# Layer 1's output projection as plain fp32 products, with stationary widths of 128, 64 and 32 columns

## The chip, the cores and the metric

The kernel runs on one core of one Trainium2 chip. The metric is the device time of one execution in microseconds (us); the time before is the median of two runs, 1154.54 us. The core's engines are named PE (TensorE, with its weight loads as a row of their own, PEld), DVE (VectorE), ACT (ScalarE), POOL (GpSimd) and SP (SyncE, whose queue issues the DMA transfers here).

## The reference, cut to what matters

Two layers of a diffusion backbone work on 512 latent and 256 context tokens of width 1024. Each layer runs two attention branches (a neighbourhood attention and a grouped-query attention) on one modulated input, gates their outputs, merges them and projects the result back:

```python
def _merge(a_att, b_att, a_z, b_z, g_a, g_b, w_o_a, w_o_b, w_out):
    o_a = (a_att * jax.nn.silu(a_z)) @ w_o_a
    o_b = (b_att * jax.nn.silu(b_z)) @ w_o_b
    merged = jax.nn.sigmoid(g_a) * o_a + jax.nn.sigmoid(g_b) * o_b
    return merged @ w_out
...
    x_new = x + gate_x * out_x
```

The change touches `merged @ w_out` of layer 1, the last layer. There only the 512 latent tokens are left: a product of 512 x 1024 by 1024 x 1024, and after it the gate and the residual sum, which is the kernel's output. All inputs are fp32.

## The kernel before, in words

Nearly all large products are done in three passes on split operands. A tile is split into `hi`, the tile rounded to the fp32r type, and `lo`, the rest; `mm3` (lines 339 to 343) then adds hi x hi, hi x lo and lo x hi in PSUM, each as a matmul of fp32r operands. The first operand of `T.matmul` after the output is the stationary one (128 rows by up to 128 columns), the second is the moving one (128 by 512 here). The sum over the 1024 inputs is made of KT = 8 steps of 128, the k tiles.

Weights come through `load_w` (lines 303 to 316): for every k tile a DMA on SP's queue (line 309) into one of three staging buffers `raw`, a cast on ACT into `whi` (line 311), and a subtraction into `wlo` (line 314), alternately on POOL and DVE for this projection (`mix_lo`). `whi` and `wlo` have 8 buffers each.

A token projection, `tok_proj` (called for each tile of 128 tokens), takes a PSUM tile of 128 x 512, runs `tok_mm` (lines 345 to 349) over the 8 k tiles with the token tile of the activations as the stationary operand and a weight tile as the moving one, and hands the result to an evacuation function.

The end of a layer stands from line 981 on:

- The projection of branch b (`o_chunks("b", ...)`), in four chunks of 256 output channels. Its weights are split tiles too and use the same `whi` and `wlo` buffers. Its evacuation `evac_b` gates the product (line 993), adds branch a (line 994), and splits the sum into the tiles `mh` (a cast on ACT, line 996) and `ml` (a subtraction on DVE, line 997). These are the merged activations, with the channels on the partitions; `mg` holds them, four channel tiles in each pair of large buffers (`big`, 9 buffers of 128 x 3072).
- The residual tiles `xt` are loaded (line 1013; four in layer 1).
- The output projection: for each half `n` of the 1024 output columns, the weights `w_out` are loaded, and for each token tile `t` (6 in layer 0, 4 in layer 1) `tok_proj` runs. The evacuation `evac_o` multiplies by the gate (line 1025) and adds the residual (line 1027) on DVE; in layer 1 the result goes to the output by a DMA (line 1029).

The order of instructions on each engine is set by a scheduler that simulates a timeline when the kernel is built: instructions that are ready in its timeline may be moved ahead of others that still wait, so products of neighbouring token tiles can be interleaved. PSUM tiles of 512 columns come from two pools, `psf` (one buffer) and `psx` (five buffers at this stage).

One place of the kernel already uses plain fp32 matmuls: `ada_part` (from line 185) computes layer 0's modulation. Its products, line 190, have a stationary tile `scol` of 32 columns and a moving weight tile of 512; four of them, each with its own k tile, go to four quarters of the partitions of one PSUM tile:

```python
        for h, w in enumerate(ws):
            for j in range(4):
                T.matmul(pt[32 * j:32 * j + 32], scol[:, 4 * h + j, :], w[:, j, :], start=h == 0, stop=h == 1)
```

`ada_part` is called four times, with 8 matmuls each. Line 655 and its neighbours transpose fp32 tiles of 128 x 128 on PE, by a product with an identity.

Of the kernel before, what the change touches and what calls it, by code (L numbers as in the profile page):

```python
# [7 lines left out]
F32 = mybir.dt.float32  # L8
# [3 lines left out]
ALU = mybir.AluOpType  # L12
# [9 lines left out]
KT = DM // 128  # L22
# [17 lines left out]
def R(ap):  # L40
    return ap.bitcast(F32R)


def F(ap):
    return ap.bitcast(F32)
# [3 lines left out]
def hybrid_kernel(es: ExitStack, tc, x, ctx, cvec, w_ada, w_ada0, small, gvec, w_in, w_o_a, w_o_b, w_out,  # L49
                  bias_int, bias_edge, rope, ident_d, out):  # L50
    nc = tc.nc
    V, S, G, T = nc.vector, nc.scalar, nc.gpsimd, nc.tensor
# [3 lines left out]
    wp = es.enter_context(tc.tile_pool(name="wp", bufs=8))  # L56
# [6 lines left out]
    def nm(s):  # L63
        uid[0] += 1
        return f"{s}_{uid[0]}"

    def big(name):
        return bigp.tile([128, 3072], F32, tag="big", name=nm(name))
# [12 lines left out]
    def open_ps(x=0, **kinds):  # L81

        if "es" in pm:
            pm["es"].close()
        pm["es"] = ExitStack()
        pm["n"], pm["i"] = x + 1, 0
        if x:
            kinds["x"] = (x, 512)
        for kind, (bufs, cols) in kinds.items():
            ps_pool(pm["es"], kind, bufs, cols)  # L90

    def psw(n=512, kind="w"):
        if kind == "w":
            kind = "f" if pm["i"] % pm["n"] == 0 else "x"
            pm["i"] += 1
        pool, cols = pm[kind]
        return pool.tile([128, cols], F32, tag=kind, name=nm("ps" + kind))[:, :n]
# [9 lines left out]
    def x_src(t):  # L107
        if t < 4:
            return x0[128 * t:128 * t + 128, :]
        return ctx0[(t - 4) * 128:(t - 3) * 128, :]  # L110
# [52 lines left out]
    def raw_tile():  # L163
        return wp.tile([128, 512], F32, tag="raw", name=nm("raw"), bufs=3)
# [67 lines left out]
    def ada_mod(l):  # L232
        mod_finish(l, ada_sum(0, 16, 2).rearrange("p (a k) v -> p a k v", a=2), 0, 8)
# [69 lines left out]
    def load_w(src, col0, n, nk, lo_eng, k0=0, own=None, bufs=8):  # L303

        pool, x = (wp, "") if own is None else (own, "x")
        res = []
        for k in range(k0, k0 + nk):
            raw = raw_tile()
            nc.sync.dma_start(raw[:, :n], src[128 * k:128 * k + 128, col0:col0 + n])
            hi = pool.tile([128, 512], F32R, tag="whi" + x, name=nm("whi"), bufs=bufs)  # L310
            S.copy(hi[:, :n], raw[:, :n])  # L311
            lo = pool.tile([128, 512], F32R, tag="wlo" + x, name=nm("wlo"), bufs=bufs)
            e = lo_eng(k)
            e.tensor_tensor(lo[:, :n], raw[:, :n], F(hi[:, :n]), ALU.subtract)  # L314
            res.append((hi, lo))
        return res

    def load_w2(src, col0, nk, lo_eng):

        res = []  # L320
        for i in range(nk // 2):
            raw = raw_tile()
            nc.sync.dma_start(raw.rearrange("p (k n) -> p k n", k=2),
                              src[256 * i:256 * i + 256, col0:col0 + 256].rearrange("(k p) n -> p k n", k=2))
            hi = wp.tile([128, 512], F32R, tag="whi", name=nm("whi"), bufs=8)
            S.copy(hi, raw)  # L326
            lo = wp.tile([128, 512], F32R, tag="wlo", name=nm("wlo"), bufs=8)
            lo_eng(i).tensor_tensor(lo, raw, F(hi), ALU.subtract)  # L328
            res += [(hi[:, c:c + 256], lo[:, c:c + 256]) for c in (0, 256)]
        return res  # L330

    pool_lo = lambda k: G
    bq_lo = lambda k: G if k % 4 == 0 else V
    mix_lo = lambda k: V if k % 2 == 1 else G
# [10 lines left out]
    def tok_mm(ps, w, n, a, t, k0, k1):  # L345
        for k in range(k0, k1):
            hi, lo = a(0, k), a(1, k)
            mm3(ps, (R(hi[:, 128 * t:128 * t + 128]), R(lo[:, 128 * t:128 * t + 128])),
                (w[k][0][:, :n], w[k][1][:, :n]), k == 0, k == KT - 1)

    def tok_proj(w, n, a, t, evac):

        ps = psw(n)
        tok_mm(ps, w, n, a, t, 0, KT)
        evac(t, ps)
        turn_late(hp["lag"])
# [31 lines left out]
    def turn_late(n):  # L388

        while len(hp["late"]) > n:  # L390
            behind(ON_PE, hp["late"].pop(0))

    def run(fill, n):
        for _ in range(min(n, len(fill))):
            fill.pop(0)()
# [80 lines left out]
    def layer(l, hx, nxt, mid):  # L476
        first = l == 0
# [59 lines left out]
        def hilo_tiles(name):  # L537
            return [big(name + part).rearrange("p (f n) -> p f n", f=4) for part in "hl"]

        def hilo(src, dst, fs):  # L540
            sv = src.rearrange("p (f n) -> p f n", f=4)
            for f in fs:
                S.copy(R(dst[0][:, f, :ntok]), sv[:, f, :ntok])
                G.tensor_tensor(R(dst[1][:, f, :ntok]), sv[:, f, :ntok], dst[0][:, f, :ntok], ALU.subtract)
# [28 lines left out]
        def tg_part(c, f, n0, n1):  # L573
            return tg[2 * (f // 4) + c].rearrange("p (f n) -> p f n", f=4)[:, f % 4, n0:n1]
# [7 lines left out]
        if first:  # L582
            w, pss = [], [psw() for t in range(6)]
# [19 lines left out]
        else:  # L603
            hp["p"] = bgp_es.enter_context(tc.tile_pool(name=f"cp{l}", bufs=1, reuse_waits="tile"))
            w = load_w(W, C_AK, 512, KT, mix_lo)
# [6 lines left out]
        w = load_w(W, C_AV, 512, KT, mix_lo)  # L612
# [5 lines left out]
        w = load_w(W, C_AQ, 512, KT, mix_lo, own=hp["p"])  # L618
# [17 lines left out]
        if True:  # L636
# [262 lines left out]
            w = load_w2(W, C_BKV, KT, mix_lo)  # L899
# [81 lines left out]
        with tc.tile_pool(name=f"mrg{l}", bufs=1, reuse_waits="tile") as mp:  # L981
            open_ps(x=5)
            extra = lambda name: mp.tile([128, 3072], F32, tag="extra", name=nm(name))
            gv = mp.tile([128, nv, DM], F32, tag="gate", name=nm("gate"), bufs=1)
            for v in range(nv):
                src = gd[l][8 * v:8 * v + 8].rearrange("k p -> (k p)").unsqueeze(0)
                nc.sync.dma_start(gv[:, v, :], src.to_broadcast([128, DM]))
            hilo(zb, gated["b"], [3])
            mg = []

            def evac_b(f, n0, n1, ps):
                a, b = tg_part(0, f, n0, n1), tg_part(1, f, n0, n1)
                V.scalar_tensor_tensor(b, b, 1.0, ps, ALU.add, ALU.mult)
                V.tensor_tensor(a, a, b, ALU.add)
                hi, lo = [m[:, f % 4, n0:n1] for m in mg[f // 4]]
                S.copy(R(hi), a)
                V.tensor_tensor(R(lo), a, hi, ALU.subtract)
            chunks = o_chunks("b", None, evac_b)
            chunks[0][0]()
            for i in range(4):  # L1000
                if i < 3:
                    chunks[i + 1][0]()
                if i % 2 == 0:
                    mg.append(hilo_tiles("m"))
                for piece in chunks[i][1]:
                    piece()

            nt = 6 if first else 4
            xv = [a.rearrange("p (t n) -> p t n", t=3) for a in (big("xt0"), extra("xt1"))]
            xts = []  # L1010
            for t in range(nt):
                xt = xv[t // 3][:, t % 3, :]
                nc.sync.dma_start(xt, x_src(t) if first else xs1[128 * t:128 * t + 128, :])
                xts.append(xt)
            a_m = lambda part, k: mg[k // 4][part][:, k % 4, :]
            bg = ada_steps(1, range(16), (1,), 2, mp) + [lambda: ada_mod(1)] if first else []
            run(bg, 1)
            per_bg = -(-len(bg) // nt)
            for n in range(2):
                w = load_w(w_out[l], 512 * n, 512, KT, mix_lo)  # L1020

                def evac_o(t, ps, n=n):
                    cs = slice(512 * n, 512 * n + 512)
                    t1 = mp.tile([128, 512], F32, tag="t1", name=nm("t1"), bufs=2)
                    V.tensor_tensor(t1, ps, gv[:, 0 if t < 4 else 1, cs], ALU.mult)
                    xt = xts[t]
                    V.tensor_tensor(xt[:, cs], xt[:, cs], t1, ALU.add)
                    if not first:
                        nc.sync.dma_start(o_lat[16 * t:16 * t + 16][:, :, cs], xt[:, cs])
                    elif n == 1:  # L1030
                        if t < 4:
                            nc.sync.dma_start(xs1[128 * t:128 * t + 128, :], xt)
                        late.append(lambda: make_hx(1, t, xt, nxt(), mp))
                late = []
                for t in range(nt):
                    tok_proj(w, 512, a_m, t, evac_o)
                    run(bg, per_bg)
                    run(late, len(late) - 1)
                run(late, len(late))
# [102 lines left out]
```

## Time and profile before

| | |
|---|---|
| runs | 1154.26 and 1154.82 us, median 1154.54 |
| profiled execution: span from the first to the last instruction | 1153.4 us (the page gives no other time of this execution) |
| span against the median of the runs | 1.1 us less |
| PE busy | 1123.0 us, 97% of the span |
| DVE, ACT, POOL busy | 809.8, 573.9, 495.0 us |
| mean granted TensorE clock | 0.998 |
| changed stage, from its first product to the end of its last | 1104.34 to 1147.86 us of the span, 43.52 us |
| tail after it | 5.54 us |

How to read it: a row of the profile names line, engine, operation and tiles (`psx<-wlo,mh` is a write to a PSUM tile that reads `wlo` and `mh`, which of them is stationary isn't said), then the stationary shape (128*128) and the moving one (128x512). Matmuls are pipelined: one starts before the one ahead of it has ended, and their ends are modelled. So a matmul's duration is not what it adds to the time; the distance from one start to the next is. A stretch is written from:to in microseconds from the span's start. All types are shown as f32 where a matmul's operand is fp32 or fp32r; the line tells which it is.

### The profile page before, as it was taken

The numbers are of one execution on the slowest core, as the hardware profiler recorded it, in microseconds if no ns is written. First come the engines' busy times: TensorE is split into PE (matmuls) and PEld (weight loads), VectorE is DVE, ScalarE is ACT, GpSimd is POOL, SyncE is SP. The second block draws the span as 40 slices with busy tenths as digits, with TensorE's granted clock in tenths as the row PEclk, the third lists the DMA queues.
The fourth block names the chain that finished last, engine by engine and source line by source line (L and its number), as shares of the span: only waits on it lengthen the run. The fifth ranks groups of instructions, "written<-read, shape, count | busy, mean of one in ns | idle before, by whom it ended". The sixth has DMA issues, their size and how long they took to land.

```text
span 1153.4 us, 17280 instructions
## 1 busy us (share of the span) xinstructions
PE 1123.0 (97%) x6078; PEld 949.0 (82%) x6078; DVE 809.8 (70%) x1508; ACT 573.9 (50%) x1167; POOL 495.0 (43%) x459
## 2 busy tenths in 40 slices
PE   5999999999999999999999999999999999999998
PEld 4688888889988888878788787888888988887786
DVE  4566688897464687688587755469787665898563
ACT  5453266666433465566330265346666445766521
POOL 3362354454375243354411126245553664465311
PEclk9999999999999999999999999999999999999999
DMA  9644222233342332470353523543332333142143
GB/s 368 195 126 137 69 85 65 72 115 97 115 130 63 107 102 73 67 276 19 121 172 101 174 74 110 176 106 113 108 105 84 110 101 101 65 173 92 63 129 92
DMA packets 88000, 134.04 MB, mean 116 GB/s; under 512 B 10629, under 2 KB 52585, under 8 KB 86249
## 3 DMA queue, kind: packets, MB, share of 16 engines
q1 hardware_dynamic: 87912, 132.94, 36.8%
q8 instruction: 48, 0.79, 0.3%
q14 instruction: 40, 0.32, 0.1%
HBM read 115.58 MB, written 17.32 MB: 115 GB/s over the span
## 4 chain that ended last, share of the span: by engine, by line
PE 83%; DVE 7%; issue 3%; POOL 2%; ACT 2%; DMA 2%; ACTq 0%; POOLq 0%; DVEq 0%
PE psx L341 12%; PE psx L343 12%; PE psx L342 12%; PE psf L341 9%; PE psf L342 9%; PE psf L343 9%; PE pst L655 5%; PE pss L704 2%; PE pss L705 2%; PE psv L959 2%; PE psv L958 1%; PE pss L781 1%; PE pst L417 1%; DVE wlo L328 1%; DVE ptl L659 1%
## 5 line engine op out<-in xcount | busy, mean ns | idle before, releaser
L659 DVE TENSOR_TENSOR ptl<-pst,pth 128x512 fp32r<-128x512 f32 (+1 forms) x176 | 116.0, 672 | 46.4 <-ACT pth L658 45.4
L658 ACT CAST pth<-pst 128x512 fp32r<-128x512 f32 (+1 forms) x176 | 99.2, 576 | 87.5 <-PE pst L655 56.3
L328 POOL TENSOR_TENSOR wlo<-raw,whi 128x512 fp32r<-128x512 f32 x68 | 95.0, 1402 | 108.9 <-ACT whi L326 87.8
L341 PE MATMUL psf<-hx,whi 128*128 128x512 f32 (+1 forms) x368 | 139.2, 378 | 0.0
L342 PE MATMUL psf<-hx,whi 128*128 128x512 f32 (+1 forms) x368 | 138.1, 375 | 0.0
L343 PE MATMUL psf<-hx,wlo 128*128 128x512 f32 (+1 forms) x368 | 137.8, 374 | 0.0
L341 PE MATMUL psx<-whi,hx 128*128 128x512 f32 (+1 forms) x368 | 137.2, 374 | 0.0
L342 PE MATMUL psx<-wlo,hx 128*128 128x512 f32 (+1 forms) x368 | 135.8, 369 | 0.0
L343 PE MATMUL psx<-whi,hx 128*128 128x512 f32 (+1 forms) x368 | 133.6, 369 | 0.0
L314 POOL TENSOR_TENSOR wlo<-raw,whi 128x512 fp32r<-128x512 f32 x44 | 60.4, 1373 | 140.4 <-ACT whi L311 123.8
L311 ACT CAST whi<-raw 128x512 fp32r<-128x512 f32 x96 | 58.7, 623 | 103.5 <-PE psx L343 38.6
L326 ACT CAST whi<-raw 128x512 fp32r<-128x512 f32 x136 | 82.5, 622 | 50.3 <-DMA raw<-in_w_in_dram 34.1
L655 PE MATMUL pst<-ident,p 128*128 128x128 f32 x640 | 99.9, 272 | 1.4 <-DVE ptl L659 0.9
L328 DVE TENSOR_TENSOR wlo<-raw,whi 128x512 fp32r<-128x512 f32 x68 | 70.2, 1033 | 28.3 <-ACT whi L326 27.8
L655 PEld LDWEIGHTS pst<-ident,p 128*128 128x128 f32 x640 | 77.7, 141 | 13.3 <-DVE ptl L659 1.6
L644 POOL TENSOR_SCALAR r<-r 128x1 f32<-128x1 f32 x64 | 23.1, 361 | 151.7 <-DVE r L639 144.1
L645 POOL TENSOR_TENSOR p<-p,r 128x512 f32<-128x512 f32 (+1 forms) x64 | 83.5, 1304 | 5.0
L341 PEld LDWEIGHTS psx<-whi,hx 128*128 128x128 f32 x368 | 69.6, 189 | 11.8 <-issue 0.8
L343 PEld LDWEIGHTS psf<-hx,wlo 128*128 128x128 f32 x368 | 69.4, 188 | 11.8
L343 PEld LDWEIGHTS psx<-whi,hx 128*128 128x128 f32 x368 | 69.4, 189 | 11.5
L342 PEld LDWEIGHTS psx<-wlo,hx 128*128 128x128 f32 x368 | 69.6, 189 | 11.0
L341 PEld LDWEIGHTS psf<-hx,whi 128*128 128x128 f32 x368 | 69.4, 189 | 10.8 <-ACT zt L502 0.2
(239 smaller groups left out, 3033.4 us busy)
## 6 DMA issues: line engine op xcount, KB each, us to landing
raw<-in_w_in_dram SPq DMA_DIRECT2D x168, 256.0 KB, 2.9
rawb<-in_w_ada_dram SPq DMA_DIRECT2D x64, 256.0 KB, 2.8
gs<-zt SPq DMA_DIRECT2D x32, 256.0 KB, 2.0
raw<-in_w_out_dram SPq DMA_DIRECT2D x32, 256.0 KB, 2.8
tg<-gs SPq DMA_DIRECT2D x4, 1536.0 KB, 7.4
rawx<-in_w_ada_dram SPq DMA_DIRECT2D x4, 1024.0 KB, 7.2
rawy<-in_w_ada_dram SPq DMA_DIRECT2D x4, 1024.0 KB, 12.2
raw<-in_w_o_a_dram SPq DMA_DIRECT2D x16, 256.0 KB, 2.7
```

Source lines behind the costliest of these rows:

```text
L311: S.copy(hi[:, :n], raw[:, :n])
L314: e.tensor_tensor(lo[:, :n], raw[:, :n], F(hi[:, :n]), ALU.subtract)
L326: S.copy(hi, raw)
L328: lo_eng(i).tensor_tensor(lo, raw, F(hi), ALU.subtract)
L341: T.matmul(ps, lhs[0], rhs[0], start=first, stop=False)
L342: T.matmul(ps, lhs[0], rhs[1], start=False, stop=False)
L343: T.matmul(ps, lhs[1], rhs[0], start=False, stop=last)
L644: G.tensor_scalar(r[:, i:i + 1], r[:, i:i + 1], 0.5, None, ALU.mult)
L645: G.tensor_tensor(p[:, c0:c1], p[:, c0:c1], r[:, i:i + 1].to_broadcast([128, c1 - c0]), ALU.mult)
L655: T.transpose(pt[:, c0:c0 + 128], src, ident)
L658: S.copy(hi[:, n0:n1], pt[:, n0:n1])
L659: V.tensor_tensor(lo[:, n0:n1], pt[:, n0:n1], F(hi[:, n0:n1]), ALU.subtract)
```

## The change

In layer 1 (`first` is false) alone:

- `evac_b` writes the merged sum as one fp32 tile `mf`, with one DVE instruction, and does not split it. `mg` holds one large buffer for four channel tiles in place of two.
- `load_full` loads the weights of the output projection as plain fp32 tiles, straight by DMA into the buffers of the tags `wlo` (even k) and `whi` (odd k). Nothing is staged, cast or subtracted.
- `full_mm` replaces `tok_proj` in the loop over the token tiles. For each k tile it runs one plain fp32 matmul for each group of `cols` stationary columns, into the partitions of PSUM that belong to these tokens. `cols` is 128 for token tile 0, 64 for tile 1 (two groups), 32 for tiles 2 and 3 (four groups each).

Layer 0 is as before. The evacuation `evac_o`, the residual loads and the output transfers are unchanged.

```diff
+    def load_full(src, col0, n, nk):
+
+        res = []
+        for k in range(nk):
+            w = wp.tile([128, 512], F32, tag="whi" if k % 2 else "wlo", name=nm("wf"), bufs=8)
+            nc.sync.dma_start(w[:, :n], src[128 * k:128 * k + 128, col0:col0 + n])
+            res.append(w)
+        return res
+
+    def full_mm(ps, w, n, a, t, cols):
+        for k in range(KT):
+            for c in range(0, 128, cols):
+                T.matmul(ps[c:c + cols], a(k)[:, 128 * t + c:128 * t + c + cols], w[k][:, :n],
+                         start=k == 0, stop=k == KT - 1)
...
             def evac_b(f, n0, n1, ps):
                 a, b = tg_part(0, f, n0, n1), tg_part(1, f, n0, n1)
                 V.scalar_tensor_tensor(b, b, 1.0, ps, ALU.add, ALU.mult)
+                if not first:
+                    V.tensor_tensor(mg[f // 4][:, f % 4, n0:n1], a, b, ALU.add)
+                    return
...
-                    mg.append(hilo_tiles("m"))
+                    mg.append(hilo_tiles("m") if first else big("mf").rearrange("p (f n) -> p f n", f=4))
...
-                w = load_w(w_out[l], 512 * n, 512, KT, mix_lo)
+                w = (load_w if first else load_full)(w_out[l], 512 * n, 512, KT, *[mix_lo][:first])
...
-                    tok_proj(w, 512, a_m, t, evac_o)
+                    if first:
+                        tok_proj(w, 512, a_m, t, evac_o)
+                    else:
+                        ps = psw(512)
+                        full_mm(ps, w, 512, lambda k: mg[k // 4][:, k % 4, :], t, (128, 64, 32, 32)[t])
+                        evac_o(t, ps)
```

## The prediction

> **What bounds the kernel now.** I read the head of the page first, then the busy time in three stretches: the end of the projection before the changed one, the changed projection itself (layer 1's output projection), and the tail.
>
> ```profile
> span 1153.4 us, 17280 instructions
> PE 1123.0 (97%) x6078; PEld 949.0 (82%) x6078; DVE 809.8 (70%) x1508; ACT 573.9 (50%) x1167; POOL 495.0 (43%) x459
> PE 83%; DVE 7%; issue 3%; POOL 2%; ACT 2%; DMA 2%; ACTq 0%; POOLq 0%; DVEq 0%
> ...
> 1084.74:1104.34 19.60, 19.60 (x89) 16.17 (x87) 14.11 (x21) 8.67 (x15) 7.17 (x6) 1.00 0.26 83
> 1104.34:1147.86 43.52, 43.52 (x193) 35.85 (x191) 18.90 (x27) 6.96 (x12) 6.47 (x5) 1.00 0.42 127
> 1147.86:1153.40 5.54, 0.16 (x1) 0.00 (x0) 1.38 (x2) 0.00 (x0) 0.00 (x0) 0.88 0.18 47
> ```
>
> The columns of the stretches are: width, then busy time with count of PE, PEld, DVE, ACT and POOL, the granted clock, the DMA share, GB/s. PE carries 83% of the chain of work that ended last, and in the changed stage PE is busy for 43.52 of 43.52 us at clock 1.00. Nothing there waits for data, DVE has 18.90 us of work and ACT 6.96. So one thing sets the time of this stage: how long TensorE needs for its products. Time that the change saves on ACT, DVE or POOL in this stage is not on the path. The products of the stage, by form:
>
> ```profile
> L342 PE MATMUL psx<-wlo,mh 128*128 128x512 f32 x56 | 21.6, 389 | 0.0
> L343 PE MATMUL psx<-whi,ml 128*128 128x512 f32 x56 | 21.6, 389 | 0.0
> L341 PE MATMUL psx<-whi,mh 128*128 128x512 f32 x56 | 21.5, 389 | 0.0
> ...
> 1145.59 0.39 PE L343 MATMUL psx<-whi,ml 128*128 128x512 f32 x1
> ...
> 1146.27 0.39 PE L343 MATMUL psx<-whi,ml 128*128 128x512 f32 x1
> ```
>
> Each line has 8 more in the other PSUM pool, which makes 3 x 64 = 192 (the stretch counts 193, one of them the tail of the stage before): 2 halves of the output columns, 4 token tiles, 8 k tiles, three passes. A matmul's 389 ns is not its price, because the next one starts before it ends; the price is the distance between starts. Three passes of one k tile take 1146.27 - 1145.59 = 0.68 us, so one takes 0.2267 us, and 192 take 43.5 us: the width of the stage.
>
> **What a plain fp32 product costs.** The kernel has such a product already. Line 190, in layer 0's modulation, multiplies two plain fp32 tiles, 32 stationary columns by 512 moving ones, four such groups side by side in one PSUM tile. That is the form of the third and fourth token tiles after the change. Its rows (four calls of the part, 8 calls of matmul in each):
>
> ```profile
> L190 PE MATMUL pst<-rawx,scol x32: 592/605/617, 12.9 to 47.6; 128*32 128x512 f32 x32
> L190 PE MATMUL pst<-rawy,scol x32: 592/592/593, 13.8 to 48.5; 128*32 128x512 f32 x32
> ...
> 30.10 0.40 PE L343 MATMUL psx<-whi,hx 128*128 128x512 f32 x1
> 30.42 0.64 PE L190 MATMUL pst<-rawx,scol 128*32 128x512 f32 x4
> ...
> 30.88 0.61 PE L190 MATMUL pst<-rawx,scol 128*32 128x512 f32 x4
> 31.31 0.61 PE L190 MATMUL pst<-rawy,scol 128*32 128x512 f32 x4
> ...
> 32.28 0.50 PE L341 MATMUL psx<-whi,hx 128*128 128x512 f32 x1
> 32.61 0.39 PE L342 MATMUL psx<-wlo,hx 128*128 128x512 f32 x1
> ```
>
> The 32 calls left 64 records, so each call is two. Four records start together at 30.42, four at 30.88, four at 31.31: the four column groups do run side by side, and a batch takes 31.31 - 30.88 = 0.43 us. That is about two passes of 0.2267, so a k tile (two batches) takes 0.86 to 0.89 us (30.42 to 31.31). I take 0.87. The record's length says the same: 592 ns against 389 for a three-pass product, 203 ns or about one pass of 512 columns more.
>
> So grouping fills the array again, and no more than that: four groups of 32 cost what one tile of 128 should cost. Against 0.68 us for three passes, the fp32 product is the dearer one: four passes in place of three.
>
> **128 and 64 stationary columns** are not in the trace as fp32 products. The nearest row for 128 is the transposition, an fp32 operand against the fp32 identity:
>
> ```profile
> 1079.90 0.60 PE L655 MATMUL pst<-ident,p 128*128 128x128 f32 x4
> ...
> L655 PE MATMUL pst<-ident,p x12: 270/272/273, 1079.9 to 1082.6; 128*128 128x128 f32 x12
> ```
>
> Four of them take 0.60 us with a last one of 0.272, so the starts are (0.60 - 0.272) / 3 = 0.109 us apart for 128 columns: 0.437 for 512, and 0.87 for the two records of a call. Lower bound: one pass for each record, 2 x 0.2267 = 0.45. Upper bound at 128: weight loads that no longer hide. The loads of the three-pass products take 35.85 / 191 = 0.188 us each and lie beside the products now; bare, they make 2 x (0.437 + 0.188) = 1.25 us of a k tile. Upper bound at 64: two groups one after the other, 1.74. I take 0.87 for both, the row nearest to them on either side of their width. For 32 columns the lower bound is the measured 0.86; the upper one is a rate at which PE gets instructions. The closest that pairs of load and product stand for long is this:
>
> ```profile
> 420.28 0.28 PE L343 MATMUL psf<-hx,wlo 128*128 128x256 f32 x1
> 420.40 0.28 PE L341 MATMUL psf<-hx,whi 128*128 128x256 f32 x1
> ```
>
> That is 0.12 us a pair. A k tile in four groups has 8 pairs, 0.96 us at this rate; line 190 ran 8 pairs in 0.89, but only in bursts of 16 that may have been queued while PE waited.
>
> **Changes of form.** Into line 190 the step is 30.42 - 30.10 = 0.32 us where 0.227 is usual; out of it, the last batch starts at about 31.74 and the next product at 32.28, 0.54 in place of 0.43, and one more step is 0.33. That is 0.1 us going in and 0.2 coming out. The stage has six changes (three passes to 128, 128 to 64, 64 to 32, back to 128, then to 64 and 32): 6 x 0.15 = 0.9 us, with 0.6 and 1.2 as ends. The Trainium skill (TensorEngine Tiling (Array Packing), section "Key Properties") speaks against the mixing of widths: changing the tiling mode drains the engine, whereas moving between tiles of a mode doesn't. It gives no price; the rows above agree with some 0.1 to 0.2 us at each change.
>
> **What else moves.** These edits I cost at nothing, and PE's full row in the stage is what hides them.
>
> ```profile
> L311 ACT CAST whi<-raw 128x512 fp32r<-128x512 f32 x16 | 9.9, 621 | 22.5 <-PE psx L343 11.5 <-DMA raw<-in_w_out_dram 8.4 <-PE psx L342 2.5
> L314 POOL TENSOR_TENSOR wlo<-raw,whi 128x512 fp32r<-128x512 f32 x8 | 11.1, 1388 | 32.9 <-ACT whi L311 32.9
> L314 DVE TENSOR_TENSOR wlo<-raw,whi 128x512 fp32r<-128x512 f32 x8 | 6.0, 749 | 11.9 <-ACT whi L311 11.9
> L997 DVE TENSOR_TENSOR ml<-tg,mh 128x512 fp32r<-128x512 f32 x8 | 6.6, 835 | 0.7 <-ACT mh L996 0.7
> L996 ACT CAST mh<-tg 128x512 fp32r<-128x512 f32 x8 | 5.0, 623 | 8.9 <-DVE tg L994 5.8 <-issue 3.0
> ```
>
> All of these go: 9.9 + 5.0 us of ACT, 11.1 of POOL, 6.0 + 6.6 of DVE. For each merged channel tile a cast and a subtraction (0.62 and 0.68 us or more) vanish ahead of its first use, so the last one is ready some 1.5 us sooner. Nothing is won by that, since PE had other products to do and did not idle. It is needed later, too: the last k tile of the first token tile comes 7 x 0.87 = 6.1 us after the stage's start. Should that cover fail, a late tile costs one or two microseconds.
>
> The 16 weight transfers of 256 KB stay. They land in the 8 + 8 buffers of the split weights and no longer in three staging buffers, so they wait for the products of the projection before, in place of a conversion:
>
> ```profile
> 1090.81 12.85 SPq L309 DMA_DIRECT2D raw<-in_w_out_dram  x6
> 1103.71 1.37 SPq L1013 DMA_DIRECT2D xt<-xs  x3
> ...
> raw<-in_w_out_dram SPq DMA_DIRECT2D x13, 256.0 KB, 3.0
> ```
>
> That projection runs 96 products, 21.8 us, until 1104.34. The buffers of the first 8 transfers come free by its middle, about 1093.4, those of the other 8 by its end. With 3.0 us to land and some queueing, the first column half has its weights by about 1098; the second has them by about 1110 and needs them 28 us after 1104.34. The four residual tiles (512 KB each) and the eight output transfers are as before, and the tail, from the last product over two DVE instructions to the output's landing, stays at 5.54 us: the last batch of four groups ends together, and its evacuation is the old one.
>
> **The sum.** Removed: 43.5 us. Added: 64 k tiles x 0.87 = 55.7, changes of form 0.9. The span goes from 1153.4 to 1153.4 - 43.5 + 55.7 + 0.9 = 1166.5 us. The page gives no time for its execution but the span; the median of the two runs, 1154.54, lies 1.1 above it, so I add 1.1: **1167.6 us**, 13.1 us or 1.1% slower.
>
> **Rivals.**
>
> *Not slower.* The 0.43 us of a batch could be the price of four streams of moving data at once, not of an fp32 record: each record one pass when it runs alone or with one neighbour. Then 128 and 64 columns cost 0.45 us a k tile and only the groups of 32 cost 0.87. One column half takes 16 x 0.45 + 16 x 0.87 = 21.1 us, both 42.2, with the changes of form 43.1 in place of 43.5: 1154.1 us. It decides at the first token tile: starts of 128 column records 0.23 us apart. For it: no such product is in the trace. Against it: a record of line 190 is itself 203 ns longer than a one-pass product, and a transposition, which has no neighbour, also takes 0.437 us for 512 columns. Chance 0.05. The Trainium skill (Perfetto Trace Analysis, section "Engine Utilization", the first note to its table) halves the array's output rate for FP32_LOW_HIGH. Read as the rate of the whole product that is 0.45 us for each k tile, an estimate that would put this rival's price on the first two token tiles; read as the rate of one of the two records it is 0.9, and line 190's 0.87 agrees with that reading only.
>
> *Two groups of 64 don't overlap.* If the 64 column form ran its groups one after the other, the second token tile would cost 16 x (1.74 - 0.87) = 13.9 us more: 1181.5. For it: no 64 column product is in the trace. Against it: four of 32 do overlap, by the same partition offsets of the output. Chance 0.09.
>
> *Late weights and mixed tiles.* If SP's queue puts the weight loads behind the three residual loads of 1103.71, the first weights land at about 1106.7 and PE waits 2.4 us; and if the order of instructions mixes token tiles of different widths, as the present one mixes tiles while merged channels are late, some 16 more changes of form cost 16 x 0.15 = 2.4: 1172.4. Chance 0.10.
>
> *Weight loads or issue bind.* Bare weight loads at 128 cost 16 x (1.25 - 0.87) = 6.1 us, and pairs at 0.12 us add 32 x (0.96 - 0.87) = 2.9 in the tiles of four groups: up to 1176.6. Chance 0.07.
>
> That the change doesn't do what it says I leave out: the diff replaces the only calls in that loop.
>
> **How the numbers follow.** The forecast has 0.69, and its own range is 1165 to 1171 (0.86 to 0.89 for each k tile, 0.6 to 1.2 for the changes of form, and a few microseconds for order). The range to hold the time is 1163 to 1178: it takes in the forecast, the mixed tiles and the weight loads (0.86 together) and leaves out the rivals at 1154.1 and 1181.5 (0.14). A change of 2%, about what a measurement of this kernel can tell from none, is 23.1 us. Slower by more than that are the groups of 64 in turn (0.09) and a piece of the last two cases if they meet (0.03): 0.12. Faster by over 2% would need more than half of the stage to go, which no case gives: 0.01. Within 2%: 0.87.
>
> **What would show it.** Right: in the changed kernel the stage between the same neighbours is 56 to 58 us wide with PE full; 128 column records start 0.43 to 0.44 us apart; groups of 64 start in pairs and of 32 in fours at that same distance; steps of 0.3 us appear only where the width changes; ACT and POOL have nothing to do in the stage; the tail is 5.5 us. Wrong: 128 column records 0.23 us apart (not slower), pairs of 64 with the second record a whole step after the first (in turn), PE idle behind a weight transfer at the stage's start, or a weight load between two products that PE waits for.

## The result and the profile after

The changed kernel takes 1170.05 us (median of two runs, 1169.24 and 1170.85) against 1154.54: a ratio of 1.0126, with a 95% interval from 1.0107 to 1.0145. It is 1.3% slower, and clear of noise. The profiled execution is the one of 1169.24 us, with a span of 1167.4.

The head of the page after:

```profile
span 1167.4 us, 17527 instructions
PE 1137.3 (97%) x6238; PEld 931.4 (80%) x6238; DVE 798.1 (68%) x1492; ACT 559.8 (48%) x1143; POOL 483.6 (41%) x451
PE 81%; DVE 8%; issue 3%; POOL 2%; DMA 2%; ACT 2%; SPq 0%; POOLq 0%; ACTq 0%; DVEq 0%
```

PE gained 14.3 us of busy time and the span grew by 14.0; DVE, ACT and POOL lost 11 to 14 us each, and the span shows nothing of it. The stretches after, with the columns of before (the second one is the changed stage):

```profile
1084.70:1104.71 20.01, 20.01 (x88) 16.56 (x89) 9.63 (x15) 1.20 (x2) 2.58 (x2) 1.00 0.75 256
...
1104.71:1162.00 57.29, 57.29 (x353) 18.26 (x351) 11.06 (x16) 0.00 (x0) 0.00 (x0) 1.00 0.18 53
1162.00:1167.40 5.40, 0.12 (x4) 0.00 (x0) 1.38 (x2) 0.00 (x0) 0.00 (x0) 0.90 0.18 49
```

The stage went from 43.52 to 57.3 us, with PE full and the clock at 1.00; ACT and POOL do nothing in it, and the tail is 0.14 us shorter. The changed line's products in the timeline of PE (start, length, tile of the first, count; a run of records of one line is merged, whatever their width):

```profile
1104.71 29.46 PE L344 MATMUL psx<-wf,mf 128*128 128x512 f32 x176
1134.10 7.13 PE L344 MATMUL psf<-wf,mf 128*128 128x512 f32 x16
1141.17 20.96 PE L344 MATMUL psx<-wf,mf 128*64 128x512 f32 x160
```

The first line is the first half of the output columns, 1134.10 - 1104.71 = 29.39 us; the second half lasts to 1162.13, less 0.16 by which a last record outlasts the usual step: 27.87. The stage is 57.26 us. The two halves do the same work, and the first takes 1.5 us more. Where it goes is seen in the weight loads of the first half (start, length, width, count, idle before):

```profile
1109.01 0.19 PEld L344 LDWEIGHTS psx<-wf,mf 128*128 128x128 f32 x1 [0.24 <-issue]
1109.95 0.19 PEld L344 LDWEIGHTS psx<-wf,mf 128*64 128x64 f32 x2 [0.76 <-issue]
1110.96 0.30 PEld L344 LDWEIGHTS psx<-wf,mf 128*128 128x128 f32 x2 [0.81 <-issue]
1112.01 0.20 PEld L344 LDWEIGHTS psx<-wf,mf 128*64 128x64 f32 x4 [0.76 <-issue]
1112.50 0.14 PEld L344 LDWEIGHTS psx<-wf,mf 128*64 128x64 f32 x2 [0.29 <-issue]
1112.92 0.14 PEld L344 LDWEIGHTS psx<-wf,mf 128*64 128x64 f32 x2 [0.29 <-issue]
1113.88 0.30 PEld L344 LDWEIGHTS psx<-wf,mf 128*128 128x128 f32 x2 [0.81 <-issue]
1114.93 0.20 PEld L344 LDWEIGHTS psx<-wf,mf 128*64 128x64 f32 x4 [0.76 <-issue]
...
1118.42 0.14 PEld L344 LDWEIGHTS psx<-wf,mf 128*64 128x64 f32 x2 [0.28 <-issue]
1118.85 0.14 PEld L344 LDWEIGHTS psx<-wf,mf 128*64 128x64 f32 x1 [0.28 <-issue]
1119.28 0.14 PEld L344 LDWEIGHTS psx<-wf,mf 128*64 128x64 f32 x1 [0.29 <-issue]
1120.23 0.16 PEld L344 LDWEIGHTS psx<-wf,mf 128*32 128x32 f32 x8 [0.81 <-issue]
```

Three things are to be seen. Inside one width the lines are 0.43 us apart, with one load at 128, two at 64, four at 32. At each change of width there is a gap of 0.76 to 0.81 us with no load, where it is 0.24 to 0.30 else. And the order mixes token tiles 0 and 1: 128, 64, 128, 64, 128, 64, so four changes more than the program's order has. At 1109.95 only two loads of 64 stand: the two records of one group without its neighbour. At 1118.85 and 1119.28 the other group's last two come alone. So the two groups of token tile 1 run one k tile apart: between these places each record stands beside one of the other group for a neighbouring k tile, which costs no more than a neighbour of the same k tile, and the eight k tiles take nine turns of 0.86 us. Four changes at 0.16 us (measured below) and the ninth turn's 0.86 make the 1.5.

### The profile page after: what moved, and what is told of

Same layout as the page of the kernel before. It is cut to its first block, busy times and chain, and to the rows that moved or that the text cites. A ratio compares the mean times of both kernels' runs of the same rounds, so it can differ in the third digit from the quotient of the medians.

```text
span 1167.4 us, 17527 instructions
## 1 busy us (share of the span) xinstructions
PE 1137.3 (97%) x6238; PEld 931.4 (80%) x6238; DVE 798.1 (68%) x1492; ACT 559.8 (48%) x1143; POOL 483.6 (41%) x451
## 4 chain that ended last, share of the span: by engine, by line
PE 81%; DVE 8%; issue 3%; POOL 2%; DMA 2%; ACT 2%; SPq 0%; POOLq 0%; ACTq 0%; DVEq 0%
PE psx L358 10%; PE psx L357 10%; PE psx L356 10%; PE psf L356 9%; PE psf L357 9%; PE psf L358 9%; PE pst L670 4%; PE psx L344 4%; PE pss L719 2%; PE pss L720 2%; PE psv L974 2%; PE pss L796 1%; PE psv L973 1%; PE pst L432 1%; DVE wlo L328 1%
## 5 line engine op out<-in xcount | busy, mean ns | idle before, releaser
L328 POOL TENSOR_TENSOR wlo<-raw,whi 128x512 fp32r<-128x512 f32 x68 | 95.0, 1401 | 108.6 <-ACT whi L326 87.5
L326 ACT CAST whi<-raw 128x512 fp32r<-128x512 f32 x136 | 82.5, 622 | 50.1 <-DMA raw<-in_w_in_dram 34.3
L314 POOL TENSOR_TENSOR wlo<-raw,whi 128x512 fp32r<-128x512 f32 x36 | 49.7, 1384 | 108.3 <-ACT whi L311 100.6
L311 ACT CAST whi<-raw 128x512 fp32r<-128x512 f32 x80 | 48.8, 623 | 82.6 <-DMA raw<-in_w_in_dram 29.5
```

## The experiments

In the results a stage's width is counted from its first product's start to 0.16 us before the last record's end (a record of 0.59 us, a step of 0.43). The theory: an fp32 product is two records of 0.43 us, whatever its width, a group of fewer than 128 columns is free only beside its neighbours, and TensorE alone sets the stage. The rivals: the width has a price of its own, or other engines and transfers set a part of the time. The kernels with one width, the one in the program's order and the one that keeps the conversions ran four times each, the other five once; those five are read by the width of the stage.

**All token tiles at one width.** The edit for 128; the kernels for 64 and 32 have that number there:

```diff
-                        full_mm(ps, w, 512, lambda k: mg[k // 4][:, k % 4, :], t, (128, 64, 32, 32)[t])
+                        full_mm(ps, w, 512, lambda k: mg[k // 4][:, k % 4, :], t, 128)
```

> All four token tiles with 128 stationary columns. Theory (an fp32 product is two records of 0.429 us at any width, and each change of width costs about 0.24 us): stage 64 x 0.858 + one change = 55.2 us against 57.3 in the changed kernel, span 1165.3 us. Rival (the width itself matters, full weight loads of 0.19 us show between products, or 32 columns are the cheaper form): stage over 57 us.

> All token tiles in two groups of 64 columns. Theory: 55.2 us for the stage, as with 128, and starts in pairs 0.429 us apart. Rival (the two groups of 64 hide only beside other widths and go in turn when they stand alone): up to 110 us.

> All token tiles in four groups of 32 columns, 512 records in a row. Theory: 55.2 us for the stage, 0.429 us for each four. Rival (instructions are issued at no more than one pair of load and product in 0.12 us): 64 x 0.96 = 61.4 us.

Measured, the timelines of PE for 128, for 64 and for 32 (the first line of the first is the last product of the projection before):

```profile
1104.86 0.39 PE L358 MATMUL psx<-gbh,wlo 128*128 128x512 f32 x1
1105.09 27.63 PE L344 MATMUL psx<-wf,mf 128*128 128x512 f32 x64
...
1139.42 20.76 PE L344 MATMUL psx<-wf,mf 128*128 128x512 f32 x48
```

```profile
1105.24 27.74 PE L344 MATMUL psx<-wf,mf 128*64 128x512 f32 x128
...
1139.62 20.82 PE L344 MATMUL psx<-wf,mf 128*64 128x512 f32 x96
```

```profile
1103.94 27.67 PE L344 MATMUL psx<-wf,mf 128*32 128x512 f32 x256
...
1138.30 20.78 PE L344 MATMUL psx<-wf,mf 128*32 128x512 f32 x192
```

128 records and 512 records take the same time: 1160.02 - 1105.09 = 54.93 us and 1158.92 - 1103.94 = 54.98; the 256 records at 64 take 1160.28 - 1105.24 = 55.04. So a batch takes 54.93 / 128 = 0.429 us at every width. The ratios to the kernel before are 1.0097 (1.0081 to 1.0112) at 128, 1.0096 (1.0080 to 1.0112) at 64, 1.0102 (1.0081 to 1.0123) at 32: one width is as good as the next, all are slower than three passes, and mixing the widths gains nothing. The issue rate does not bind, with 512 pairs of load and product in a row, 0.107 us each.

The spans are 1165.4, 1165.7 and 1164.4; the last is 1 us shorter because its stage starts a microsecond earlier. That microsecond is from the start of the run: in the first 50 us the granted clock is 1.00 there, and 0.97 in the kernels for 128 and 64 and in the changed kernel. The first line is the kernel for 32, with 206 products by then, the second the changed kernel, with 203:

```profile
0.00:50.00 50.00, 37.01 (x206) 24.75 (x207) 26.07 (x60) 24.39 (x44) 18.37 (x25) 1.00 0.78 302
```

```profile
0.00:50.00 50.00, 37.11 (x203) 25.28 (x204) 26.17 (x60) 24.40 (x44) 17.97 (x25) 0.97 0.78 301
```

So the stage's width is the better measure for a microsecond than the span.

**The program's order.** `behind` ties each TensorE instruction to the one before it in the program.

```diff
-                        full_mm(ps, w, 512, lambda k: mg[k // 4][:, k % 4, :], t, (128, 64, 32, 32)[t])
+                        behind(ON_PE, lambda: full_mm(ps, w, 512, lambda k: mg[k // 4][:, k % 4, :], t, (128, 64, 32, 32)[t]))
```

> The changed kernel with TensorE's instructions of this stage in the order of the program (token tile after token tile), widths as in the change. Theory: 6 changes of width in place of 10, so 4 x 0.24 = 1.0 us less: stage 56.3 us, span 1166.4. Rival (the mixing covered a merged channel tile that is late): TensorE idles at the first token tile, no gain or 1 to 2 us more.

```profile
1104.94 27.91 PE L344 MATMUL psx<-wf,mf 128*128 128x512 f32 x176
1132.79 7.13 PE L344 MATMUL psf<-wf,mf 128*128 128x512 f32 x16
1139.85 20.96 PE L344 MATMUL psx<-wf,mf 128*64 128x512 f32 x160
```

The stage is 1160.65 - 1104.94 = 55.71 us, 1.55 less than in the changed kernel and all of it in the first half (27.85 for 29.39). TensorE doesn't wait for a merged tile. The gain is larger than the 1.0 I expected and the price of a change is smaller: against 54.93 at one width, five changes cost 0.78, 0.16 us each. My 0.24 had put the split pair on the changes.

**The price of a change of width.**

```diff
         for k in range(KT):
+            cols = 32 if k % 2 else 128
             for c in range(0, 128, cols):
```

(and `behind`, as above.)

> Every token tile with 128 columns for even k tiles and four groups of 32 for odd ones, in program order: 63 changes of width inside the stage where the all-128 kernel has none. Theory (0.15 us for a change, the gap between the program-order kernel and the all-128 one shared among 5 changes): 54.9 + 63 x 0.15 = 64.4 us for the stage, 61 to 68 with 0.1 to 0.2 each. Rival (a change costs 0.38 us, the whole excess of the changed kernel's mixed stretch over four changes): 78.9 us.

```profile
1104.57 32.79 PE L345 MATMUL psx<-wf,mf 128*128 128x512 f32 x160
...
1145.49 24.69 PE L345 MATMUL psx<-wf,mf 128*128 128x512 f32 x120
```

```profile
1105.51 0.16 PEld L345 LDWEIGHTS psx<-wf,mf 128*32 128x32 f32 x8 [0.76 <-DVE tg L1009]
1106.51 0.30 PEld L345 LDWEIGHTS psx<-wf,mf 128*128 128x128 f32 x2 [0.84 <-DVE mf L1011]
1107.57 0.16 PEld L345 LDWEIGHTS psx<-wf,mf 128*32 128x32 f32 x8 [0.76 <-issue]
```

A k tile now takes 1.00 us at 32 and 1.06 at 128 where 0.858 is usual. The stage is 1170.02 - 1104.57 = 65.45 us, 10.5 more than at one width: 0.17 for each of the 63 changes. That is a little over the theory's 0.15 and inside its range; the rival's 0.38 falls.

**One group without neighbours.**

```diff
-            for c in range(0, 128, cols):
-                T.matmul(ps[c:c + cols], a(k)[:, 128 * t + c:128 * t + c + cols], w[k][:, :n],
-                         start=k == 0, stop=k == KT - 1)
+            for c in range(0, 128 if k == 0 else 32, 32):
+                T.matmul(ps[c:c + 32], a(k)[:, 128 * t + c:128 * t + c + 32], w[k][:, :n],
+                         start=k == 0, stop=k == (KT - 1 if c == 0 else 0))
```

> All token tiles in groups of 32, but from the second k tile on only the first group of the four is computed (the other three keep the product of the first k tile alone, so three quarters of the projection is left out). Theory (a record takes two passes of the array whether it has neighbours or not): the stage keeps its 55 us although it has 256 + 896 / 4... records fewer: 704 of 1024 are gone. Rival (0.429 us is what four streams of moving data need together, one alone takes one pass): 8 x 0.86 + 56 x 0.45 = 32 us.

The counts in this text are wrong: of 512 records 176 are left, as the next rows show. The times don't hang on it.

```profile
L344 PE MATMUL psx<-wf,mf x154: 592/592/617, 1104.6 to 1159.2; 128*32 128x512 f32 x154
...
L344 PE MATMUL psf<-wf,mf x22: 592/592/617, 1131.3 to 1138.6; 128*32 128x512 f32 x22
```

With a third of the records the stage is 1159.2 + 0.43 - 1104.6 = 55.0 us, the same. A record takes 0.43 us alone as among four; the rival of shared streams falls here.

**Group after group.** The all-64 kernel with its loops exchanged (and `behind`):

```diff
-        for k in range(KT):
-            for c in range(0, 128, cols):
+        for c in range(0, 128, cols):
+            for k in range(KT):
```

> Two groups of 64 columns as in the all-64 kernel, but all 8 k tiles of the first group come before those of the second, so that a group never has its neighbour beside it. Theory (a lone group costs as much as a full array, which is what a split pair cost in the changed kernel): 128 x 0.858 = 109.8 us for the stage, span about 1220. Rival (the engine looks ahead and overlaps the groups anyway): 55 us.

```profile
1110.53 0.14 PEld L344 LDWEIGHTS psx<-wf,mf 128*64 128x64 f32 x1 [0.29 <-issue]
1110.96 0.20 PEld L344 LDWEIGHTS psx<-wf,mf 128*64 128x64 f32 x3 [0.29 <-issue]
1111.38 0.20 PEld L344 LDWEIGHTS psx<-wf,mf 128*64 128x64 f32 x2 [0.23 <-issue]
1111.82 0.19 PEld L344 LDWEIGHTS psx<-wf,mf 128*64 128x64 f32 x2 [0.23 <-issue]
1112.30 0.14 PEld L344 LDWEIGHTS psx<-wf,mf 128*64 128x64 f32 x1 [0.29 <-issue]
```

```profile
1105.75 42.24 PE L344 MATMUL psx<-wf,mf 128*64 128x512 f32 x125
...
1159.16 31.77 PE L344 MATMUL psx<-wf,mf 128*64 128x512 f32 x93
```

Neither 110 us nor 55: the stage is 1190.77 - 1105.75 = 85.0 us, the span 1196.2. One group loads and runs alone for most of its 16 records, and around each border between groups two run side by side for a few steps. A group takes 5.2 us to the next one's start (1105.75, 1110.96, 1116.16), 12 steps of 0.43 in place of 16. So TensorE does look ahead here, but only about four records far: a group that is free has to stand close to its neighbour in the program.

**Half of the products.** The changed kernel's loop over every second k tile, which leaves out half of the sum:

```diff
-        for k in range(KT):
+        for k in range(0, KT, 2):
...
-                         start=k == 0, stop=k == KT - 1)
+                         start=k == 0, stop=k == KT - 2)
```

> The changed kernel with every second k tile left out (half of the projection's sum). Theory (TensorE's passes alone set the stage): half the batches, 32 x 0.858 = 27.5 us and up to 2.3 for changes and a pair that is split, 28 to 30 us, span about 1139. Rival (weights, evacuation or output transfers stand close behind): the stage stays above 32 us with TensorE idle in it.

```profile
1107.49 15.38 PE L344 MATMUL psx<-wf,mf 128*128 128x512 f32 x88
...
1126.43 10.66 PE L344 MATMUL psx<-wf,mf 128*64 128x512 f32 x80
```

The stage is 29.4 us, in the expected 28 to 30. The span is 1142.4 and not 1139, as the stage began 2.8 us later than in the changed kernel; the first 50 us had a granted clock of 0.93. Nothing else comes near, even with the stage at half its length.

**The conversions kept.**

```diff
             nc.sync.dma_start(w[:, :n], src[128 * k:128 * k + 128, col0:col0 + n])
+            hi, lo = raw_tile(), raw_tile()
+            S.copy(R(hi), w)
+            mix_lo(k).tensor_tensor(R(lo), w, hi, ALU.subtract)
             res.append(w)
...
-                    V.tensor_tensor(mg[f // 4][:, f % 4, n0:n1], a, b, ALU.add)
+                    m = mg[f // 4][:, f % 4, n0:n1]
+                    V.tensor_tensor(m, a, b, ALU.add)
+                    S.copy(R(a), m)
+                    V.tensor_tensor(R(b), m, a, ALU.subtract)
```

> The changed kernel's plain fp32 products with the old conversions done all the same: each weight tile is cast on ACT and subtracted on POOL or DVE, each merged channel tile is cast and subtracted too, and nothing reads the results. Theory (the conversions were off the path, so dropping them brought nothing): stage 57 us as in the changed kernel, or 55.7 where the order happens not to mix widths; span 1166 to 1168. Rival (the dropped conversions hid a part of the products' loss): 1 to 4 us slower than the changed kernel, with TensorE idle in the stage.

```profile
1105.50 29.46 PE L347 MATMUL psx<-wf,mf 128*128 128x512 f32 x176
...
1141.95 20.96 PE L347 MATMUL psx<-wf,mf 128*64 128x512 f32 x160
```

The stage is 1162.75 - 1105.50 = 57.25 us, to 0.01 us that of the changed kernel, with all conversions back. Its ratio to before is 1.0136 (1.0119 to 1.0153), with the changed kernel's 1.0126 inside. Dropping the conversions gained nothing in the stage.

**Two passes.** From the kernel before, with the pass hi x lo left out of this projection:

```diff
-                    tok_proj(w, 512, a_m, t, evac_o)
+                    if first:
+                        tok_proj(w, 512, a_m, t, evac_o)
+                    else:
+                        ps = psw(512)
+                        for k in range(KT):
+                            hi, lo = [R(m[:, 128 * t:128 * t + 128]) for m in (a_m(0, k), a_m(1, k))]
+                            T.matmul(ps, hi, w[k][0][:, :512], start=k == 0, stop=False)
+                            T.matmul(ps, lo, w[k][0][:, :512], start=False, stop=k == KT - 1)
+                        evac_o(t, ps)
```

> The kernel before with two passes in place of three in layer 1's output projection (the product of the rounded activations with the weights' rest is left out). Theory (time is passes of TensorE: 0.2267 us for an fp32r pass, 0.2146 for one of the four of an fp32 product): 128 x 0.2267 = 29.0 us for the stage, span 1139. Rival (the conversions of the weights, 0.62 us of ACT and 0.7 to 1.3 us of DVE or POOL each, become the bound as soon as TensorE is quicker): a stage over 31 us with TensorE idle.

```profile
1106.34 0.39 PE L1042 MATMUL psx<-whi,mh 128*128 128x512 f32 x1
...
1134.90 0.39 PE L1042 MATMUL psx<-whi,mh 128*128 128x512 f32 x1
1135.12 0.39 PE L1043 MATMUL psx<-whi,ml 128*128 128x512 f32 x1
```

The stage is 1135.12 + 0.23 - 1106.34 = 29.0 us, as expected: 128 passes at 0.2267, and the conversions still don't bind. With two passes at 29.0, three at 43.5 and fp32 products at 54.9, the stage follows what TensorE has to run. Its one run took 1143.15 us, 12.1 less than the median of the kernel before beside it (1155.29); what it gives up for that is the product of the rounded activations with the weights' rest.

## Why the prediction was right, step by step

*TensorE's products alone set the stage.* Shown: the half of the products makes the stage about half as long (29.4 us of 57.26), and the conversions change nothing.

*Removed, 43.5 us.* As said: the stage before was 43.52.

*An fp32 product of 0.87 us at every width.* The mechanism was right, and the row of line 190 was the one to go by: its batches of 0.43 came back at 32, 64 and 128. The size is 0.858, so 64 k tiles are 54.9 us and not 55.7; I had rounded up to the span that holds the entry into the form.

*Six changes of form at 0.15 us, 0.9.* The price is right, 0.16 to 0.17 between two fp32 widths. The entry from three passes to 128 columns costs nothing (at 128 the first fp32 product starts 0.23 us after the last product before), the other five cost 0.78. The sign it named, steps of 0.3 us where the width changes, came only where three passes meet a narrower group (0.32 us into the kernel with 64 columns); between two fp32 widths the extra lies on steps of 0.43, and a k tile takes 1.00 to 1.06 us in place of 0.858. The Trainium skill's rule in TensorEngine Tiling (Array Packing), "Key Properties", is that a change of the tiling mode drains TensorE and a change of tile alone doesn't. The traces agree: at a change of width no load starts for 0.76 to 0.84 us, and within one width it is 0.24 to 0.30 in the changed kernel.

*Edits at nothing.* Right for the conversions and for the merged tiles. The weights were in time: these are the transfers of the SP queue after, eight for each half:

```profile
1086.55 8.06 SPq L337 DMA_DIRECT2D wf<-in_w_out_dram  x8
...
1098.11 7.38 SPq L337 DMA_DIRECT2D wf<-in_w_out_dram  x8
```

The first eight are issued before 1094.7, ten microseconds ahead of the stage.

*What the sum left out.* Mixed token tiles stood among the rivals, at 2.4 us for 16 more changes together with a late start. No weight was late, and of the mixing 1.5 us came: four changes (0.6) and a pair of groups pulled apart (0.86), which I had not thought of. So the sum was 0.8 too high in one place and 1.5 too low in another: 57.26 - 43.52 = 13.7 us for the stage in place of 13.1. That the miss is smaller than either error is luck. With 0.4 us that the stage began later and 0.1 that the tail is shorter, the span grew by 14.0.

*From span to time.* I added 1.1 us, the distance of the profiled span before to the median of other runs. In the runs of the changed kernel the time is 1.8 us over the span in each (1169.24 for 1167.4, 1170.85 for 1169.0), and in a run of the kernel before beside the first experiments too (1155.27 for 1153.5). Of the 2.5 us by which 1167.6 fell short of the median, 0.7 come from there, 0.9 from the span (1167.4 for 1166.5), and 0.8 are half the distance to the second, longer run.

*The rivals.* Not slower: fell, with records of 128 columns 0.43 us apart. Two groups of 64 in turn: fell for a pair that stands together, 55.0 us at all 64; where a group has no neighbour within reach its records go in turn, and the two groups of a k tile would take four steps of 0.43, the 1.74 us of that rival. Weight loads or issue: fell, 54.9 us with full loads and 55.0 with 512 pairs.

## What to carry to other kernels

Where TensorE is full, as in this stage, the time is what its products cost: an fp32 product of 512 columns took 0.858 us, three passes on split operands took 0.68, and what fp32 saved, the conversions, lay on engines that the stage did not wait for. Cutting the stationary columns into groups gave the array's width back, no more, and only where a group of other columns stood close by in the order of the program. Choose one width for a stage (2.3 us of the 15.5 here), or at least hold the order if the scheduler may mix widths and pull groups apart (1.5 of these 2.3).

No version tried that computes the whole projection beats the kernel before; the best with fp32 products is one width for all tiles, 1.0% slower.

## What the runs showed of the hardware that was not expected

- A lone group of 32 or 64 columns took as long as a full array, 0.43 us a record. With the loops exchanged, TensorE reached about four records ahead for a neighbour in another column group: 12 steps in place of 16 for a group.
- The trace shows an fp32 product as two records of 0.429 us. Counted as two passes a record, as the prediction does, that is 0.2146 us a pass, less than the 0.2267 of an fp32r pass; neither the count of four passes nor the cause of the difference was tested.
- In the kernels with fp32 products the stage began at 1103.94 us where the granted clock of the first 50 us was 1.00, at 1104.6 to 1105.8 where it was 0.97, and at 1107.49 where it was 0.93. That the clock is the cause is read from this agreement alone.
